# Seven block products where eight stood, in both squared-ReLU layers of a two-layer decoder trunk

## The chip, the cores and the metric

The kernel runs on one core of a Trainium2 chip. The metric is the device time of one execution in microseconds (us), as the median of several runs; 2941.45 us before the change (three runs, 2940.11 to 2944.54). Everything is float32. The matrix products run on TensorE (PE in the profile) in three passes: both operands are split into a high part (float32 rounded to the engine's float32r format) and a low part (the remainder), and high by high, high by low and low by high are added in the accumulator (PSUM).

## What is computed

Two layers over 1024 tokens of width 1024. Each has a token mixer (mLSTM with RG-LRU in layer 0, sliding-window attention in layer 1), a cross attention into 256 memory tokens, and the squared-ReLU layer that the change touches:

```python
D_MODEL = 1024; SEQ = 1024; D_FF = 4 * D_MODEL; DEPTH = 2

def squared_relu_mlp(u, w1, w2):
    return jnp.square(jax.nn.relu(u @ w1)) @ w2

for l in range(DEPTH):
    ...                                   # token mixer, then cross attention
    u = squared_relu_mlp(rms_norm(h, g_ff_pre[l]), w_ff1[l], w_ff2[l])
    h = h + rms_norm(u, g_ff_post[l])
```

## The kernel before

The whole trunk is one program. A tile has 128 partitions. The normalised input of a stage is kept transposed (channels on partitions) as u[half], one pair of tiles (`uh`, `ul`: high, low) for each half of 512 tokens, each of 8 blocks of 128 channels.

**Pools.** On-chip memory is cut into pools that live through the whole program: `xp` with 35 slots of 520 floats per partition for temporaries (`X`), `up` with four tiles of 8 by 512 (`U`), `hp` with four row tiles of 1024 (`H`), `wp` with three slots for raw weights (tag `wr`) and five for split weights (tag `w`), and eight accumulator banks in two pools, `pg` (three, `G`) and `pt` (five, `T`). A weight tile is loaded by `load_raw` (L354) and split by `split` (L210): ScalarE copies the high part (L211), VectorE subtracts it to get the low one (L212).

**Order.** Each engine runs its instructions in one order, which a list scheduler makes from the program's order and its own durations when the kernel is built: an instruction whose operands and slot are there goes ahead of an earlier one that has to wait. Two chains are fixed by hand with `ordered`: all TensorE instructions stand in program order (key "pe"), and so do the weight loads (key "w"). What has to come between matmuls is placed by a counter of estimated TensorE time, `clock`: `defer(d, fn)` puts a piece of work d us later, and `pe(us)` advances the counter and runs what is due. `ready(u)` runs all pieces that are left until u is complete.

**The squared-ReLU layer before** (`mlp`, L700 to L757). The hidden width is taken in eight chunks of 512 (`for c in range(8)`). In each, `proj_T` (L387) makes four hidden tiles for each token half, 24 matmuls of 128x128 by 128x512 each (8 channel blocks, three passes) into one G bank; then ScalarE takes the ReLU (L717), VectorE multiplies it with the accumulator to square it (L718), and `split` makes `hh` and `hl`, which stay on the chip in X slots. Then `tile_out` adds the chunk's share of the output for 8 token tiles by 2 column halves, 12 matmuls each, with `hh`/`hl` as the stationary operand; VectorE adds the bank to the running sum `acc` (L738; a ScalarE copy, L736, in the first chunk). The last chunk's products are mixed with the output's normalisation: after each tile `post_half` (L333: ScalarE sums squares, GpSimd multiplies by the gain, L337) and, after the second half of a token tile, `post_norm` (L339: `rsqrt` on VectorE, L253 to L265, two residual updates, L345, and the store). In layer 0, `after` starts the next layer's `pre_norm` (L305) for the first four token tiles.

In both layers that makes 8 x 4 x 2 x 24 = 1536 matmuls in the first product and 8 x 16 x 12 = 1536 in the second.

`pre_norm` sums squares, scales, and after a planned delay transposes a token tile on TensorE (`transposed`, L287, L86 in the trace), multiplies by the gain (L296, `ut`), and splits into `uh` (ScalarE, L299) and `ul` (GpSimd, L300). The layer's second half of tokens is normalised this way while the first chunk's products of the first half run.

Of the kernel before, what the change touches and what calls it, by code (L numbers as in the profile page):

```python
# [10 lines left out]
F32 = mybir.dt.float32  # L11
# [17 lines left out]
NX = 35  # L29
NH = 4  # L30
XW = 520
# [28 lines left out]
def trunk(ctx: ExitStack, tc, a, out, stop=99):  # L60
# [32 lines left out]
    up = ctx.enter_context(tc.tile_pool(name="up", bufs=NU))  # L93
    hp_ = ctx.enter_context(tc.tile_pool(name="hp", bufs=NH))
    xp = ctx.enter_context(tc.tile_pool(name="xp", bufs=NX))
# [3 lines left out]

    ctr = [0]  # L100
# [87 lines left out]
    def X(shape=(P, HALF), dt=F32, n="x"):  # L188
        assert int(np.prod(shape[1:])) <= XW
        return xp.tile(list(shape), dt, tag="x", name=nm(n))  # L190
# [4 lines left out]
    def U(shape=(P, 8, HALF), n="u"):  # L195
        return up.tile(list(shape), F32R, tag="u", name=nm(n))
# [29 lines left out]

    cst = cp.tile([P, 288], F32, name="cst")
# [74 lines left out]

    left = {}

    def pre_norm(h, g, u, t, delay, where=None):  # L305
# [10 lines left out]
        def rest(un):  # L316
            transposed(un, [(g, u[0][:, :, c], u[1][:, :, c])])
            left[id(u)] -= 1
# [63 lines left out]
    def mm3(ps, lh, ll, rh, rl, start, stop):  # L382
        mm(ps, lhsT=lh, rhs=rh, start=start, stop=False)
        mm(ps, lhsT=lh, rhs=rl, start=False, stop=False)
        mm(ps, lhsT=ll, rhs=rh, start=False, stop=stop)
# [313 lines left out]

    def mlp(l, u, hsrc, hdst, after):  # L700

        W1, W2 = a["w_ff1"][l], a["w_ff2"][l]
        acc = [[None, None] for _ in range(8)]
        wpool[0] = 0
        g = None
        for c in range(8):
            hid = [[None, None] for _ in range(4)]
            ng = 4 if c == 0 else 2
            for n0 in range(0, 4, ng):
                ws = [load_w(w_cols(W1, (4 * c + n0 + j) * P), (8, P)) for j in range(ng)]  # L710
                for half in range(2):
                    if c == 0:
                        ready(u[half])
                    for j in range(ng):
                        ps = proj_T(ws[j], u[half])
                        r = H(n="rl")[:, 0:HALF]
                        act(out=r, in_=ps, func=AF.Relu)  # L717
                        vec.tensor_tensor(out=r, in0=ps, in1=r, op=ALU.mult)  # L718
                        hh, hl = X(dt=F32R, n="hh"), X(dt=F32R, n="hl")
                        split(hh, hl, r)  # L720
                        hid[n0 + j][half] = (hh, hl)
                        pe(0)

            def w2(n):
                return [load_w(w_rows(W2, 4 * c + 2 * q, 2, n * HALF, HALF), (2, HALF)) for q in range(2)]

            def tile_out(t, n, ws):
                lhs = []
                for k in range(4):
                    hh, hl = hid[k][t // 4]  # L730
                    s = slice((t % 4) * P, (t % 4 + 1) * P)
                    lhs.append((hh[:, s], hl[:, s]))
                ps = proj_lhs(ws, lhs)
                if c == 0:
                    acc[t][n] = X(n="acc")
                    act(out=acc[t][n], in_=ps, func=AF.Copy)  # L736
                else:
                    vec.tensor_tensor(out=acc[t][n], in0=ps, in1=acc[t][n], op=ALU.add)  # L738
                pe(0)

            if c < 7:
                for n in range(2):
                    ws = w2(n)
                    for t in range(8):
                        tile_out(t, n, ws)
            else:
# [7 lines left out]
                for t, n in order:  # L754
# [3 lines left out]
                    if n == 1:  # L758
                        h = post_norm(acc[t], ss, hsrc, hdst, t)
                        if after is not None:  # L760
                            after(t, h)
# [761 lines left out]
```

## Time and profile before

| | |
|---|---|
| median of three runs | 2941.45 us (2940.11 to 2944.54) |
| the profiled execution's own time | 2938.32 us |
| its span, first to last instruction | 2936.5 us |
| mean granted TensorE clock | 0.982 of full speed |
| TensorE matmuls busy | 2816.4 us (96%), 13518 instructions |
| VectorE busy | 1617.2 us (55%) |
| ScalarE busy | 1139.1 us (39%) |
| GpSimd busy | 548.8 us (19%) |
| moved | 274.29 MB, mean 93 GB/s |

Views that are quoted below. The page's part 5 and the lists of groups give line, engine, operation, output<-inputs (for a matmul the moving operand first, then the stationary one), the count, then the busy time in us, the mean ns of one, the engine's idle time before them and what ended it. The timeline gives start and duration in us, and in brackets the idle time of the engine before the instruction and what ended it. Windows give the stretch, its length, the busy us of PE, PEld (weight loads), DVE (VectorE), ACT (ScalarE) and POOL (GpSimd) with their instruction counts, the granted clock, the DMA share and GB/s.

The busy time of matmuls overlaps between neighbours: one is shown as 0.39 us long, and the next starts before it ends. The pace is read from start to start. The squared-ReLU layer of layer 0 runs from 831.82 us to about 1553 us, that of layer 1 ends the program.

### The profile page before, as it was taken

What the parts mean: (1) busy time and instruction counts of PE and PEld (TensorE: products, weight loads), DVE (VectorE), ACT (ScalarE), POOL (GpSimd) and SP (SyncE); (2) the same over time, 40 slices, a digit from 0 to 9 for tenths busy, and PEclk for the clock granted to TensorE, in tenths of its full rate; (3) what the DMA queues carried; (4) which work ended last, traced back from release to release, by engine and by line L of the source; (5) the groups of instructions that cost most, each with busy time, mean ns of one, the idle gap of its engine ahead of it and who ended that gap; (6) DMA issues with size and microseconds to landing.
All of it is one profiled execution on the core that took longest, in us unless ns stands there. A gap on an engine that the chain in (4) does not pass through costs nothing. (4 is left out here: it accounts for less than half of the span.)

```text
span 2936.5 us, 35526 instructions
## 1 busy us (share of the span) xinstructions
PE 2816.4 (96%) x13518; PEld 2340.3 (80%) x13518; DVE 1617.2 (55%) x3168; ACT 1139.1 (39%) x2271; POOL 548.8 (19%) x442
## 2 busy tenths in 40 slices
PE   8999999999999999999998889879999999999998
PEld 8988778878788888888877668668888888888886
DVE  7776586656662333333367966986655233333336
ACT  5455454445443112221134764754544311122212
POOL 1351243522110000000024451641211000000003
PEclk9999999899999999999999899989999999999999
DMA  8633542234331111111124154034432111111113
GB/s 255 192 90 105 176 129 79 87 132 166 97 110 56 44 43 58 44 44 57 44 92 153 50 158 154 26 94 163 146 101 94 44 52 49 43 53 48 44 50 115
DMA packets 265754, 274.29 MB, mean 93 GB/s; under 512 B 11784, under 2 KB 200688, under 8 KB 265584
## 3 DMA queue, kind: packets, MB, share of 16 engines
q1 hardware_dynamic: 265584, 272.03, 29.2%
q8 instruction: 106, 1.74, 0.2%
q14 instruction: 64, 0.52, 0.1%
HBM read 234.24 MB, written 37.75 MB: 93 GB/s over the span
## 5 line engine op out<-in xcount | busy, mean ns | idle before, releaser
L82 PE MATMUL g<-uh,w 128*128 128x512 f32 x3200 | 1009.6, 392 | 1.6 <-ACT uh L299 1.6
L82 PEld LDWEIGHTS g<-uh,w 128*128 128x128 f32 x3200 | 602.3, 188 | 126.2 <-ACT uh L299 2.5
L82 PE MATMUL g<-w,hh 128*128 128x512 f32 x2048 | 642.5, 395 | 1.4 <-DVE acc L738 1.4
L212 DVE TENSOR_TENSOR w<-wr,w 128x1024 fp32r<-128x1024 f32 x344 | 439.8, 1280 | 350.7 <-ACT w L211 349.6
L82 PE MATMUL g<-ul,w 128*128 128x512 f32 x1600 | 624.7, 390 | 1.7 <-POOL ul L300 1.7
L211 ACT ACTIVATE w<-wr 128x1024 fp32r<-128x1024 f32 x344 | 362.7, 1056 | 583.0 <-PE g L82 512.2
L82 PEld LDWEIGHTS g<-w,hh 128*128 128x128 f32 x2048 | 384.5, 188 | 92.0 <-DVE acc L738 1.8
L82 PE MATMUL g<-w,hl 128*128 128x512 f32 x1024 | 404.0, 395 | 0.0
L82 PEld LDWEIGHTS g<-ul,w 128*128 128x128 f32 x1600 | 301.2, 188 | 62.5 <-POOL ul L300 2.3
L738 DVE TENSOR_TENSOR acc<-g,acc 128x512 f32<-128x512 f32 x224 | 154.4, 689 | 299.7 <-PE g L82 298.3
L718 DVE TENSOR_TENSOR rl<-g,rl 128x512 f32<-128x512 f32 x128 | 88.5, 692 | 379.1 <-ACT rl L717 379.1
L337 POOL TENSOR_TENSOR acc<-acc,gain 128x512 f32<-128x512 f32 x32 | 44.5, 1396 | 1335.6 <-ACT junk L274 1335.6
L717 ACT ACTIVATE rl<-g 128x512 f32<-128x512 f32 x128 | 76.4, 597 | 427.9 <-PE g L82 425.2
L82 PEld LDWEIGHTS g<-w,hl 128*128 128x128 f32 x1024 | 192.4, 188 | 45.7
L300 POOL TENSOR_TENSOR ul<-ut,uh 128x512 fp32r<-128x512 f32 x96 | 136.3, 1440 | 403.0 <-ACT uh L299 401.9
L82 PE MATMUL g<-w,uh 128*128 128x512 f32 (+1 forms) x640 | 173.6, 361 | 10.7 <-DVE w L212 4.8
L82 PE MATMUL g<-w,pTh 128*128 128x512 f32 x512 | 161.1, 396 | 0.5 <-ACT pTh L211 0.5
L82 PEld LDWEIGHTS g<-w,uh 128*128 128x128 f32 x640 | 111.9, 194 | 25.7 <-DVE w L212 5.1
L82 PE MATMUL g<-w,ul 128*128 128x512 f32 (+1 forms) x320 | 114.0, 356 | 0.0
L212 DVE TENSOR_TENSOR hl<-rl,hh 128x512 fp32r<-128x512 f32 x128 | 89.3, 698 | 44.2 <-ACT hh L211 44.2
L82 PEld LDWEIGHTS g<-w,pTh 128*128 128x128 f32 x512 | 95.0, 188 | 21.7 <-ACT pTh L211 1.0
L82 PE MATMUL g<-w,pTl 128*128 128x512 f32 x256 | 101.2, 395 | 0.0
(326 smaller groups left out, 3820.7 us busy)
## 6 DMA issues: line engine op xcount, KB each, us to landing
wr<-in_w_ff SPq DMA_DIRECT2D x128, 512.0 KB, 3.9
h<-h SPq DMA_DIRECT2D x100, 512.0 KB, 3.7
wr<-in_ev_w_in SPq DMA_DIRECT2D x48, 512.0 KB, 3.6
wr<-in_w_xkv SPq DMA_DIRECT2D x32, 512.0 KB, 4.7
wr<-in_w_xq SPq DMA_DIRECT2D x32, 512.0 KB, 3.9
wr<-memv SPq DMA_DIRECT2D x32, 512.0 KB, 3.8
wr<-in_od_w_qkv SPq DMA_DIRECT2D x24, 512.0 KB, 4.3
h<-in_x SPq DMA_DIRECT2D x16, 512.0 KB, 4.4
```

The source lines that it names most:

```text
L82: ins = nc.tensor.matmul(*ar, **kw)
L211: act(out=h, in_=src, func=AF.Copy)
L212: (eng or vec).tensor_tensor(out=l, in0=src, in1=f(h), op=ALU.subtract)
L300: pool.tensor_tensor(out=ul[:, q], in0=t, in1=f(uh[:, q]), op=ALU.subtract)
L337: eng.tensor_tensor(out=dst, in0=y, in1=g[:, c], op=ALU.mult)
L717: act(out=r, in_=ps, func=AF.Relu)
L718: vec.tensor_tensor(out=r, in0=ps, in1=r, op=ALU.mult)
L738: vec.tensor_tensor(out=acc[t][n], in0=ps, in1=acc[t][n], op=ALU.add)
```

## The change

Both products of `mlp` become a 2x2 block scheme with seven block products and shared sums (Winograd's form of Strassen's scheme). The two blocks of the token dimension are the halves u[0] and u[1]; channels and hidden columns are cut in two as well.

- **First product.** 16 steps of two hidden tiles. A step loads two raw tiles (one into `wr`, the other into an H slot), splits two weight blocks as they are (`direct`), makes four sums of weight blocks on VectorE and splits five blocks (`sums`), and runs seven products of 12 matmuls (`product`). The four results are put together in the accumulator where two products share a bank (`more=True`: the second product adds to a bank that was read in between) and on VectorE. ReLU and square are two ScalarE instructions in place.
- **Sums of the input.** `transposed_sum` makes the first four blocks of u[1] hold a sum of three blocks from the start; `t_sum` makes the three other sums of the input, on VectorE and ScalarE, once per layer at step 0.
- **The hidden layer goes through memory.** The four blocks of the hidden layer and their sums (four more VectorE instructions) make seven left operands, which are stored to a DRAM tile `hid` (seven stores of 256 KB a step) and loaded back in the second product (`lefts`: two loads of 512 KB and a split for each block product).
- **Second product.** Four steps of seven products of 48 matmuls (4 token tiles by 4 blocks by three passes). Four blocks of W2 of 1 MB each are loaded a step; the right operands are three of them and four sums, split by `right`. `gather` adds banks to 20 running sums.
- **The output's normalisation** stands behind the last product, in a loop over eight token tiles, where it was mixed with the last chunk's products before; tiles 4 to 7 take two more VectorE additions each, tiles 0 to 3 one.
- **Pools.** `x` and `u` are opened and closed by phase: in the first product `t` (six tiles) and ten X slots take the old X pool's place, in the second `hl` (four tiles) and `b` (six) take the place of `u`, with 22 X slots. X slots are 520 floats wide up to layer 0's squared-ReLU layer and 512 from there on.

The diff, cut to its core ("..." marks what is left out):

```diff
-NX = 35
...
+NX = 34
...
-XW = 520
+XW = (520, 512)
+NX1, NX2 = 10, 22
...
+    def open_pool(key, n, side):
+        ctr[0] += 1
+        stage_pools[key] = tc.alloc_tile_pool(name=f"{key}{ctr[0]}", bufs=n, side=side, reuse_waits="tile")
+    def close_pool(*keys):
+        for key in keys:
+            stage_pools.pop(key).release()
...
+    def transposed_sum(un, g, u, first, c):
...
+        act(out=u[0][:, 4:8, c], in_=ts[1], func=AF.Copy)
+        pool.tensor_tensor(out=u[1][:, 4:8, c], in0=ts[1], in1=f(u[0][:, 4:8, c]), op=ALU.subtract)
+        s = ts[0]
+        vec.tensor_tensor(out=s, in0=ts[1], in1=s, op=ALU.subtract)
+        for b in first:
+            vec.tensor_tensor(out=s, in0=s, in1=f(b[:, 0:4, c]), op=ALU.add)
+        act(out=u[0][:, 0:4, c], in_=s, func=AF.Copy)
+        vec.tensor_tensor(out=u[1][:, 0:4, c], in0=s, in1=f(u[0][:, 0:4, c]), op=ALU.subtract)
...
+    def mm3(ps, lh, ll, rh, rl, start, stop, more=False):
...
+    hid = dp.tile([7, 16 * P, HALF], F32, name="hid")
...
+        def pair_raw(i):
...
+                ordered("w", nc.sync.dma_start(out=r, in_=w_rows(W1, 4 * j, 4, 2 * i * P, 2 * P)))
...
+        def direct(raws):
...
+            for j in range(2):
+                split(w[:, 0, j], w[:, 1, j], raws[j][:, :, 0:P])
...
+        def sums(raws):
...
+            s1 = X((P, 4, P), F32, "s1")
+            tt(s1, a21, a22, add)
+            tt(a21, a11, a21, sub)
+            tt(a11, s1, a11, sub)
+            tt(a12, a12, a11, sub)
...
+        def product(ps, w, j, b, k0, more=False):
...
+        def squared_relu(x, src):
+            act(out=x, in_=src, func=AF.Relu)
+            act(out=x, in_=x, func=AF.Square)
...
+        ready(u[0])
+        first = 2
...
+        ready(u[1])
+        close_pool("x")
+        xw[0] = HALF
+        open_pool("t", 6, "left")
+        open_pool("x", NX1, "left")
...
+        def t_sum(x, kx, y, ky):
...
+            h, lo = (stage_pools["t"].tile([P, 4, HALF], F32R, tag="t", name=nm("t")) for _ in range(2))
+            for k in range(4):
+                d, e = X(n="d"), X(n="e")
+                tt(d, f(x[0][:, kx + k]), f(y[0][:, ky + k]), sub)
+                tt(e, f(x[1][:, kx + k]), f(y[1][:, ky + k]), sub)
+                tt(d, d, e, add)
+                split(h[:, k], lo[:, k], d)
+            return h, lo
...
+        for i in range(16):
...
+            w23, w4a, w1 = sums(raws)
+            if i >= first:
+                b1 = G("b1")
+                product(b1, wa, 0, u[0], 0)
+                p1 = X(n="p1")
+                act(out=p1, in_=b1, func=AF.Copy)
+            b2 = G("b2")
+            product(b2, w23, 0, u[1], 0)
+            u2 = X(n="u2")
+            tt(u2, b2, p1, add)
+            pe(0)
+            if i >= first:
+                product(b1, wa, 1, u[0], 4, True)
+                c11 = X(n="c11")
+                squared_relu(c11, b1)
                 pe(0)
-            if c < 7:
+            if i == 0:
+                ts.append(t_sum(u[1], 0, u[0], 0))
+                ts.append(t_sum(u[1], 4, u[1], 0))
+                ts.append(t_sum(u[0], 4, u[1], 0))
+            t3, t1, t4 = ts
+            b3, b4 = T("b3"), T("b4")
+            product(b3, w23, 1, t3, 0)
+            c22 = X(n="c22")
+            tt(c22, b3, u2, add)
+            pe(0)
+            product(b4, w1, 0, t1, 0)
+            c21 = X(n="c21")
+            tt(c22, b4, c22, add)
+            squared_relu(c22, c22)
+            pe(0)
+            product(b3, w4a, 1, t4, 0, True)
+            tt(c21, b3, u2, add)
+            squared_relu(c21, c21)
+            pe(0)
+            product(b4, w4a, 0, u[1], 4, True)
+            c12 = u2
+            tt(c12, b4, u2, add)
+            squared_relu(c12, c12)
+            pe(0)
+            s = [H("s")[:, 0:D] for _ in range(2)]
+            s1, s2, s3, s4 = (s[j // 2][:, (j % 2) * HALF : (j % 2 + 1) * HALF] for j in range(4))
+            tt(s1, c12, c22, add)
+            tt(s2, s1, c11, sub)
+            tt(s3, c11, c12, sub)
+            tt(s4, c21, s2, sub)
+            for x, src in enumerate((c11, c21, s4, c22, s1, s2, s3)):
+                store(x, i, src)
+        close_pool("x", "t", "u")
+        open_pool("x", NX2, "left")
+        open_pool("hl", 4, "right")
+        open_pool("b", 6, "right")
+        def big(key, n, dt=F32):
...
+        def gather(key, t, ps):
...
+                acc[key, t] = X(n="acc")
+                act(out=acc[key, t], in_=ps, func=AF.Copy)
+            else:
+                tt(acc[key, t], ps, acc[key, t], add)
...
+        W2v = W2.rearrange("(i e q) n -> e q i n", e=2, q=P)
+        for c in range(4):
...
+                    b = big("b", "braw")
+                    ordered("w", nc.sync.dma_start(out=b, in_=W2v[e, :, 4 * c : 4 * c + 4, n * HALF : (n + 1) * HALF]))
+                    blocks.append(b)
+            b11, b12, b21, b22 = blocks
...
+            def right(src):
+                h, lo = big("hl", "th", F32R), big("hl", "tl", F32R)
+                split(h, lo, src)
+                return h, lo
...
+            def lefts(x):
+                h, lo = (wp.tile([P, 4, HALF], F32R, tag="w", name=nm("sh"), bufs=NW) for _ in range(2))
...
+                    nc.sync.dma_start(out=r, in_=hid[x, r0 : r0 + 2 * P, :].rearrange("(i q) t -> q i t", q=P))
+                    split(h[:, 2 * j : 2 * j + 2], lo[:, 2 * j : 2 * j + 2], r)
+                return h, lo
...
+            pa = banks("pa")
+            for t in products(0, right(b11), pa):
+                gather("u", t, pa[t])
+                pe(0)
+            t1, t2 = big("b", "t1"), big("b", "t2")
+            tt(t1, b12, b11, sub)
+            tt(t2, b22, t1, sub)
+            pb = banks("pb")
+            for t in products(5, right(t2), pb):
+                gather("u", t, pb[t])
+                pe(0)
+            r21 = right(b21)
+            tt(b21, b21, t2, sub)
+            tt(b12, b22, b12, sub)
+            for t in products(1, r21, pa, True):
+                gather("11", t, pa[t])
+                pe(0)
+            pb = banks("pb")
+            for t in products(4, right(t1), pb):
+                gather("22", t, pb[t])
+                pe(0)
+            pa = banks("pa")
+            for t in products(6, right(b12), pa):
+                gather("22", t, pa[t])
+                pe(0)
+            for t in products(2, right(b22), pb, True):
+                gather("12", t, pb[t])
+                pe(0)
+            for t in products(3, right(b21), pa, True):
+                gather("21", t, pa[t])
+                pe(0)
+        close_pool("b", "hl")
+        if after is not None:
+            open_pool("u", NU, "right")
+        g = gain(a["g_ff_post"][l], True)
+        sy = small(16, "sy", 1)
+        for t in range(8):
+            ss = sy[:, 2 * t : 2 * t + 2]
+            keys = ("11", "12") if t < 4 else ("21", "22")
+            y = [acc[key, t % 4] for key in keys]
+            for n in range(2):
+                if keys[n] != "11":
+                    tt(y[n], y[n], acc["u", t % 4], add)
+                post_half(y[n], y[n], g, ss, n, pool)
+            h = post_norm(y, ss, hsrc, hdst, t)
+            if after is not None:
+                after(t, h)
+            pe(N1)
+        if after is None:
+            drain()
+            close_pool("x")
+        else:
+            close_pool("x")
+            xw[0] = XW[1]
+            open_pool("x", NX, "left")
```

## Rows read from the trace of the kernel before

**Rows 1.** The page, part 1: busy us, share of the span, instructions.

```profile
PE 2816.4 (96%) x13518; PEld 2340.3 (80%) x13518; DVE 1617.2 (55%) x3168; ACT 1139.1 (39%) x2271; POOL 548.8 (19%) x442
```

**Rows 2.** Windows: busy us per engine (instructions), granted clock, DMA share, GB/s.

```profile
50.00:100.00 50.00, 50.00 (x422) 50.00 (x421) 37.65 (x68) 26.50 (x39) 9.27 (x6) 1.00 0.94 285
900.00:950.00 50.00, 50.00 (x220) 40.83 (x219) 11.33 (x13) 16.54 (x24) 0.00 (x0) 1.00 0.17 53
1565.00:1600.00 35.00, 34.77 (x157) 28.85 (x158) 26.55 (x72) 12.79 (x33) 10.64 (x14) 0.91 0.54 184
1650.00:1700.00 50.00, 37.40 (x177) 30.43 (x176) 45.72 (x113) 37.35 (x107) 19.04 (x17) 0.84 0.28 96
```

**Rows 3.** The page, part 5: groups: busy us, mean ns, idle before.

```profile
L82 PE MATMUL g<-uh,w 128*128 128x512 f32 x3200 | 1009.6, 392 | 1.6 <-ACT uh L299 1.6
...
L212 DVE TENSOR_TENSOR w<-wr,w 128x1024 fp32r<-128x1024 f32 x344 | 439.8, 1280 | 350.7 <-ACT w L211 349.6
...
L738 DVE TENSOR_TENSOR acc<-g,acc 128x512 f32<-128x512 f32 x224 | 154.4, 689 | 299.7 <-PE g L82 298.3
...
L337 POOL TENSOR_TENSOR acc<-acc,gain 128x512 f32<-128x512 f32 x32 | 44.5, 1396 | 1335.6 <-ACT junk L274 1335.6
```

**Rows 4.** Timeline, PE, first product, layer 0: start us, us, instruction.

```profile
1103.31 0.39 PE L82 MATMUL g<-ul,w 128*128 128x512 f32 x1
...
1122.35 0.39 PE L82 MATMUL g<-ul,w 128*128 128x512 f32 x1
```

**Rows 5.** Timeline, PE, second product (layer 1).

```profile
2895.60 0.40 PE L82 MATMUL g<-w,hl 128*128 128x512 f32 x1
...
2916.55 0.40 PE L82 MATMUL g<-w,hl 128*128 128x512 f32 x1
```

**Rows 6.** Timeline, PE, output projection of the mixer, U tiles stationary.

```profile
622.04 0.39 PE L82 MATMUL g<-w,yl 128*128 128x512 f32 x1
...
636.32 0.39 PE L82 MATMUL g<-w,yl 128*128 128x512 f32 x1
```

**Rows 7.** Timeline, ACT, POOL, DVE: last tiles of the second half, layer 0.

```profile
834.63 0.58 ACT L274 ACTIVATE junk<-g 128x512 f32<-128x512 f32 x1
...
858.20 2.52 POOL L300 TENSOR_TENSOR ul<-ut,uh 128x512 fp32r<-128x512 f32 x2 [1.91 <-ACT uh L299]
...
847.87 1.28 DVE L296 TENSOR_TENSOR ut<-tr,col 128x512 f32<-128x512 f32 x2
```

**Rows 8.** Timeline, PE, start of the layer, layer 0.

```profile
831.82 0.39 PE L82 MATMUL g<-uh,w 128*128 128x512 f32 x1
...
858.17 0.50 PE L82 MATMUL g<-uh,w 128*128 128x512 f32 x1 [0.81 <-ACT uh L299]
```

**Rows 9.** Timeline, PE, the last matmul of the program.

```profile
2924.23 0.40 PE L82 MATMUL g<-w,hl 128*128 128x512 f32 x1
```

**Rows 10.** Timeline, DVE, one output normalisation of the cross attention.

```profile
816.67 0.20 DVE L257 TENSOR_SCALAR rs<-sy 128x1 f32<-128x1 f32 x1
...
818.57 1.42 DVE L345 SCALAR_TENSOR_TENSOR h<-y,rs,h 128x512 f32<-128x512 f32 x2
```

**Rows 11.** Timeline, DVE, two like instructions of one rsqrt.

```profile
1549.11 1.20 DVE L264 SCALAR_TENSOR_TENSOR rs<-rs 128x1 f32<-128x1 f32 x1
...
1553.10 0.16 DVE L264 SCALAR_TENSOR_TENSOR rs<-rs 128x1 f32<-128x1 f32 x1
```

**Rows 12.** Timeline, PE, end of the layer in layer 0.

```profile
1526.83 1.27 PE L86 MATMUL tr<-cst,un 128*128 128x128 f32 x8 [1.79 <-ACT junk L274]
...
1555.41 0.73 PE L82 MATMUL g<-w,uh 128*128 128x512 f32 x2 [2.26 <-DVE acc L738]
...
1565.23 0.79 PE L82 MATMUL g<-w,uh 128*128 128x512 f32 x1 [4.75 <-DVE w L212]
```

**Rows 13.** The page, part 6: DMA issues, KB each, median us to landing.

```profile
wr<-in_w_ff SPq DMA_DIRECT2D x128, 512.0 KB, 3.9
```

**Rows 14.** Waits of the DMA queue: waiter, releaser, us in total, times, longest.

```profile
SPq L359 <- DVE w L212: 1907.5, 272, 50.1
```

More of the change, by code (lines that the diff above doesn't have):

```diff
@@ new lines, in wtile @@
+        def wtile(n):
+            return wp.tile([P, 2, 2, 4, P], F32R, tag="w", name=nm(n), bufs=NW)
+        def direct(raws):
+            w = wtile("w")
+            for j in range(2):
+                split(w[:, 0, j], w[:, 1, j], raws[j][:, :, 0:P])
+            return w
+        def sums(raws):
+            (a11, a21), (a12, a22) = [(r[:, :, 0:P], r[:, :, P : 2 * P]) for r in raws]
+            s1 = X((P, 4, P), F32, "s1")
[3 more added lines that the diff above has]
+            tt(a12, a12, a11, sub)
+            out = []
+            for r in raws:
+                w = wtile("w")
+                split(w[:, 0], w[:, 1], r.rearrange("p k (b n) -> p b k n", b=2))
+                out.append(w)
+            w = wtile("w1")
+            split(w[:, 0, 0], w[:, 1, 0], s1)
+            return out + [w]
@@ new lines, in product, with store @@
+        def product(ps, w, j, b, k0, more=False):
+            for k in range(4):
+                mm3(
+                    ps, w[:, 0, j, k], w[:, 1, j, k], b[0][:, k0 + k], b[1][:, k0 + k], k == 0 and not more, k == 3, more
+                )
+                if k < 3:
+                    pe(0.68)
+                else:
+                    clock[0] += 0.68
+        def squared_relu(x, src):
+            act(out=x, in_=src, func=AF.Relu)
+            act(out=x, in_=x, func=AF.Square)
+        def store(x, i, src):
+            nc.sync.dma_start(out=hid[x, i * P : (i + 1) * P, :], in_=src)
@@ new lines, in mlp @@
+        ready(u[0])
+        first = 2
+        pre = []
+        for i in range(first):
+            raws = pair_raw(i)
+            pre.append([raws, direct(raws), G("b1")])
+        p1s, c11s = H("p1"), H("c11")
+        for i in range(first):
+            product(pre[i][2], pre[i][1], 0, u[0], 0)
+            pre[i].append(p1s[:, i * HALF : (i + 1) * HALF])
+            act(out=pre[i][3], in_=pre[i][2], func=AF.Copy)
+            pe(0)
+        for i in range(first):
+            product(pre[i][2], pre[i][1], 1, u[0], 4, True)
+            pre[i].append(c11s[:, i * HALF : (i + 1) * HALF])
+            squared_relu(pre[i][4], pre[i][2])
+            pe(0)
@@ new lines, in mlp @@
+        ts = []
+        for i in range(16):
+            if i < first:
+                raws, wa, b1, p1, c11 = pre[i]
+            else:
+                raws = pair_raw(i)
+                wa = direct(raws)
+            w23, w4a, w1 = sums(raws)
[13 more added lines that the diff above has]
+                squared_relu(c11, b1)
+                pe(0)
+            if i == 0:
[30 more added lines that the diff above has]
+                store(x, i, src)
@@ L764, in trunk @@
+        if after is None:
+            drain()
+            close_pool("x")
+        else:
+            close_pool("x")
+            xw[0] = XW[1]
+            open_pool("x", NX, "left")
     W_in = a["ev_w_in"][0]
@@ L1457, in trunk @@
                 in_steps(rope_tables(), 3, 3.5)
-            cross(l, half, ux[half], hm, hxr, lambda t, h, u=u: pre_norm(h, gf, u, t, UD, "x"), None if half else mid)
+            cross(l, half, ux[half], hm, hxr, lambda t, h, u=u, first=uf[0] if half else None: pre_norm(h, gf, u, t, UD, "x", first), None if half else mid)
         if stop == 2 + 3 * l:
```

121 lines of the change are left out of this document (59 added, 62 removed).

## The prediction, made before the changed kernel was run

> **What bounds the kernel now.** I read the shares first: TensorE is busy 96% of the span, the next engine 55% [rows 1]. Then the windows of 50 us: inside a squared-ReLU layer TensorE has 50.00 of 50 busy at clock 1.00, while VectorE has 11.3 and DMA a share of 0.17 [rows 2]. So the layer is bound by the number of matmuls times their pitch, and a matmul fewer gives its whole pitch back, as long as nothing else starves TensorE. The groups say the same: 3200 matmuls of one kind waited 1.6 us in all [rows 3]. Other stages look different: at 1650 to 1700 us VectorE is busy 45.7 of 50, TensorE 37.4, and the clock falls to 0.84 [rows 2]. The question is how much of the new layer looks like that.
>
> **Pitch.** First product: from 1103.31 to 1122.35 us stand 84 matmuls, 19.04 us, 0.2267 each [rows 4]. Second product: 2895.60 to 2916.55, 90 matmuls, 20.95 us, 0.2328 each [rows 5]. The longer pitch goes with a stationary operand in an X slot of 520 floats: with a U tile as the stationary one, 63 matmuls take 14.28 us, 0.2267 [rows 6]. The new second product takes its stationary operand from a `w` slot, as the first does, so I use 0.2267 there too; bounds 0.2267 and 0.2328.
>
> **What is removed.** Per layer 2 x 1536 matmuls: 1536 x 0.2267 + 1536 x 0.2328 = 705.8 us. After: 16 x 7 x 12 = 1344 and 4 x 7 x 48 = 1344, so 2688 x 0.2267 = 609.4. Gain 96.4 a layer, 193 in all (88 a layer from the missing products, 8 from the pitch, so 177 if that does not come).
>
> **Steady work of VectorE.** A 512-float VectorE instruction takes 0.69 us alone [rows 3], and 0.60 behind another one: two take 1.28 [rows 7]. A 1024-float subtraction takes 1.28 [rows 3]. A step of the first product has 16 of 512 floats (two of the direct split, four weight sums, the split of the third weight tile, five additions of banks, four sums of hidden blocks) and two of 1024: 16 x 0.67 + 2 x 1.28 = 13.3 us beside 84 x 0.2267 = 19.0 of TensorE. A step of the second product has 28 additions of banks (0.69), 14 splits of 1024 (1.28), and 7 splits and 4 sums of 2048 floats, which the trace does not have: 4 x 0.60 = 2.40 to 2 x 1.28 = 2.56; I take 2.45. Sum 19.3 + 17.9 + 27.0 = 64 us beside 76 of TensorE. Both fit, but at 70% and 84%, where it is 23% now. [...] DMA has 1 MB of weights and 1.8 MB of stores per 19 us, then 4 MB and 7 MB per 76 us: some 150 GB/s, where the core has moved 285 [rows 2]. I charge the steady part 4 us a layer for the first product (0 to 16) and 3 for the second (0 to 10).
>
> **The start of the layer, the largest cost.** Now the last block of u[1] is complete at 858.20 + 2.52 = 860.7 us, 29 us after the first matmul at 831.82, and TensorE hardly waits, since four 24-matmul groups of the first half cover it; two gaps of 0.8 us are left, one is shown [rows 7, 8]. After the change only four products (48 matmuls, 10.9 us) and the transposes (3 us) stand ahead of the wait, so TensorE is out of work at 846. The sums in `transposed_sum` add four VectorE instructions a tile, but the products' planned distance no longer delays the last tile, whose input came at 834.63 [rows 7]: I take 858 (852 to 862). From then on VectorE has the weight sums of step 0 (5.5 us), and the three `t_sum`: 48 instructions of 0.60 to 0.69, 31 us. TensorE's order is fixed, so it follows the blocks as they come: the sixth product of step 0 ends at about 898, the seventh at 901, and step 1 waits for its own weight sums until 903. By then 9 products (24.5 us) and 3 us of transposes are done in 71 us: 43 idle, less the old 1.7. Some of the 11 us of weight sums fits into VectorE's earlier gaps: **38 us a layer** (25 if all of it does and u[1] comes at 852, 48 if none and 862).
>
> **Between the products.** W2's blocks (1 MB, 3.7 us at 285 GB/s [rows 2]) go to places that `u` held, and must be split (a ScalarE copy, then 2.45 on VectorE, together about 4.4) before the first product. If the first block's place was u[0]'s, the load is hidden and 4 us stay; if u[1]'s, load and split stand bare and the second product waits for three more blocks: 17. I take **10 a layer**.
>
> **The output's normalisation.** Before, it lay under the last chunk's matmuls; the program ended 11.9 us after the last matmul's end at 2924.6 [rows 9]. A token tile costs VectorE 1.9 us of rsqrt and 1.42 of updates [rows 10] and one or two additions, about 4.3, and GpSimd two multiplications of 1.4 [rows 3], while which VectorE is held up: one instruction of an rsqrt took 1.20 us beside GpSimd's, 0.16 without [rows 11]. I take 5.6 a tile. Tiles 0 to 3 can start when the sixth product's banks are added, so about two of eight fit under the seventh; six remain: 33.6 and the store 3, 36.6. **Layer 1: +24** (13 to 31). In layer 0 four tiles must also pass `pre_norm` (rsqrt, scaling, two multiplications: 3.7 each on VectorE) before the next layer's first matmul, behind five or six output tiles: 38 us (27 to 48). Before, that place had idle gaps of 12.6 us in seven pieces, three are shown [rows 12], and 4 us of transposes now hide in the wait: **layer 0: +21** (10 to 31).
>
> **Clock.** After 4.75 idle us before 1565.23 [rows 12] the stretch 1565 to 1600 was granted 0.91, which is 35 x 0.09 = 3.2 us [rows 2]. Four or five new places: **12** (0 to 20).
>
> **Sum.** 2 x 38 + 2 x 10 + 2 x 7 + 24 + 21 + 12 = 167. Against the profiled execution's 2938.3: 2938.3 - 193 + 167 = 2912. That execution lies 3.1 below the median, so **2915 us**.
>
> **Rivals.**
> *VectorE starves the first product (slower).* Three times a step a product adds to a bank that VectorE or ScalarE has to read first, and only one other product, 2.7 us, lies between; before, banks rotated and the groups did not wait [rows 3]. If a split of 1.28 us stands ahead of the two VectorE readings and the weights come late, 3.7 us a step are lost: 32 x 3.7 = 118, less the 8 counted: 3025. It decides from (2941 - 2915 + 8)/32 = 1.1 us a step. For it: 70% busy, splits that wait for ScalarE. Against it: the scheduler's order lets the readings go first. Chance 0.2. [...]
> *The gaps are filled (faster).* The lower ends: 2 x 25 + 2 x 4 + 10 + 13 and 6 of clock are 87, which gives 2938.3 - 193 + 87 + 3 = 2835 with no steady charge; a quarter of the way back to the forecast 2855. For it: none of that work needs TensorE, and the scheduler may put it into gaps. Against it: `t_sum` alone keeps VectorE 31 us, with 11 us of products to fill them. Chance 0.22.
> *The round trip through memory is not hidden (slower).* Loads stand on the same queue as stores that wait for VectorE; if each step's load (3.9 us [rows 13]) and split (2.3) followed the step before, 28 x 6.2 = 174: 3090. Against it: now loads wait for a free slot 1907 us in all, so they run far ahead [rows 14]. Chance 0.08.
> *The gain is eaten up (no change).* If the costs come to 193, 26 us more than I sum, say 47 at each start and 14 before each second product, the result is 2941; this lies within the forecast's own spread.
>
> **How the numbers follow.** Forecast 0.5 (2885 to 2955), of which 0.36 is faster, 0.08 within and 0.06 slower by more than 0.2% (5.9 us, about what a measurement can tell from no change). The faster rival adds 0.22, the starving one 0.01 within and 0.19 slower, the memory one 0.08: faster 0.58, same 0.09, slower 0.33. The range leaves out the memory rival and the far half of the starving one: 2845 to 2990.
>
> **What would show it.** In each layer's start VectorE near full for some 40 us while TensorE idles until 858 and is then fed in pieces; after it 220 matmuls per 50 us at clock 1.00 in both products, the second product's pitch at 0.227; a gap of 4 to 17 us before the first matmul of the second product; some 36 us after the last matmul of the program. The forecast is wrong if windows inside the first product show fewer than 210 matmuls per 50 us, if the gap at the start is under 25 or over 50, or if the tail is below 25.

## The result and the profile after

The changed kernel takes 3188.05 us (median of 4 runs, 3184.13 to 3190.69) against 2940.78 before on the same chip (2938.90 to 2944.54): ratio 1.0838, 95% interval 1.0819 to 1.0857. It is slower by 247 us, where 2915 was forecast. The profiled execution took 3187.12 us, its span is 3185.3.

Part 1 of the page, shares, answering [rows 1]:

```profile
PE 2772.4 (87%) x12750; PEld 2238.4 (70%) x12750; DVE 2096.9 (66%) x3672; ACT 1389.1 (44%) x2535; POOL 536.3 (17%) x434
```

TensorE has 768 matmuls fewer, as the change says, but its busy time fell by 44 us only and its idle time grew by more than 290. Windows of 50 us (busy us per engine with instructions, granted clock, DMA share, GB/s), answering [rows 2]; the first is the start of layer 0's first product, the second its middle, the third the second product, the fourth the end of layer 0:

```profile
850.00:900.00 50.00, 25.03 (x58) 12.50 (x56) 45.67 (x73) 15.05 (x24) 4.44 (x3) 0.61 0.06 21
1000.00:1050.00 50.00, 38.75 (x150) 29.86 (x149) 24.90 (x35) 17.35 (x26) 0.00 (x0) 0.86 0.34 116
1350.00:1400.00 50.00, 50.00 (x216) 40.27 (x215) 32.18 (x25) 24.88 (x27) 0.00 (x0) 1.00 0.48 162
1650.00:1700.00 50.00, 22.73 (x92) 18.25 (x92) 43.52 (x110) 19.05 (x48) 25.46 (x20) 0.66 0.44 150
```

The second product is full. The middle of the first product is not: 150 matmuls in 50 us where the forecast wanted 220, and VectorE has 25 of 50. So it isn't a lack of VectorE time. Part 5 of the page (groups: busy us, mean ns, idle before and who ended it) names the releaser; before, the 3200 matmuls of this kind waited 1.6 us in all [rows 3]:

```profile
L83 PE MATMUL b<-uh,w 128*128 128x512 f32 x1024 | 379.6, 443 | 192.5 <-ACT w L222 189.4
```

The timeline of one step (start us, us, engine, line; in brackets the idle time before and its end), TensorE, VectorE and ScalarE around 1010 us:

```profile
1011.69 0.40 PE L83 MATMUL b<-uh,w 128*128 128x512 f32 x1
1017.67 0.79 PE L83 MATMUL b<-uh,w 128*128 128x512 f32 x1 [5.58 <-ACT w L222]
1018.26 0.63 PE L83 MATMUL b<-ul,w 128*128 128x512 f32 x1
...
1009.32 0.69 DVE L756 TENSOR_TENSOR u<-b,u 128x512 f32<-128x512 f32 x1 [2.11 <-PE b L83]
1011.37 0.69 DVE L756 TENSOR_TENSOR s<-u,c 128x512 f32<-128x512 f32 x1 [1.36 <-ACT u L809]
...
1013.31 0.69 DVE L756 TENSOR_TENSOR s<-c,s 128x512 f32<-128x512 f32 x1
1013.91 0.68 DVE L756 TENSOR_TENSOR s<-wr,wr 128x512 f32<-128x512 f32 x1
...
1015.84 0.69 DVE L756 TENSOR_TENSOR wr<-s,wr 128x512 f32<-128x512 f32 x1
...
1012.90 0.63 ACT L222 ACTIVATE w<-wr 128x512 fp32r<-128x512 f32 x1 [1.56 <-DMA wr<-in_w_ff]
1016.56 2.00 ACT L222 ACTIVATE w<-wr 128x1024 fp32r<-128x1024 f32 x2 [2.54 <-DVE wr L756]
```

Here is the loss. The step's last product ends; VectorE adds its bank (1009.32), ScalarE squares, VectorE makes the four sums of hidden blocks (1011.37 to 1014.00), and only then, back to back, the weight sums of the next step (from 1013.91), whose split on ScalarE ends at 1017.6. TensorE has meanwhile only the one product that needs no sum, 2.7 us, until 1011.9, and starts again at 1017.67. From one start to the next 5.98 us pass in place of 0.23, and the matmuls behind the wait come at 0.43 to 0.67 us for some 4 us more. In layer 0 such a wait comes in each of the last 14 steps of the first product, every 27.1 to 27.3 us (the last start before it is at 930.15, 957.24, 984.45, 1011.69 ...), where 84 matmuls are 19.4. TensorE's granted clock is 0.50 of full speed from 1017.70 to 1021.70, and 0.86 in the window of 1000 to 1050.

Two causes are possible: the place of the weight sums on VectorE's list, or the load that they read. SyncE's queue, same step:

```profile
1005.85 3.04 SPq L812 DMA_DIRECT2D hid<-c  x2
1008.99 0.38 SPq L765 DMA_DIRECT2D wr<-in_w_ff  x1
1012.10 3.22 SPq L812 DMA_DIRECT2D hid<-s  x4
```

The load issued at 1008.99 stands behind stores that wait for ScalarE, and lands just before 1012.90, where ScalarE picks it up; the weight sums that read it start at 1013.91. The two causes lie 1 us apart, and the profile alone can't say which one counts.

The other places where TensorE waits: the start of the layer (868.67 to 912.51, where step 1 begins), between the products, the end of layer 0; then the last matmul (answering [rows 8, 9, 12]).

```profile
868.67 0.80 PE L83 MATMUL b<-uh,w 128*128 128x512 f32 x1 [15.61 <-ACT w L222]
...
903.13 2.47 PE L83 MATMUL b<-t,w 128*128 128x512 f32 x5 [5.49 <-DVE c L756]
...
912.51 0.50 PE L83 MATMUL b<-uh,w 128*128 128x512 f32 x1 [0.84 <-ACT w L222]
...
1324.18 0.80 PE L83 MATMUL pa<-th,sh 128*128 128x512 f32 x1 [14.56 <-ACT th L222]
...
1642.57 0.40 PE L83 MATMUL pa<-th,sh 128*128 128x512 f32 x1
1661.56 1.97 PE L87 MATMUL tr<-cst,un 128*128 128x128 f32 x8 [18.59 <-ACT junk L287]
...
1681.79 1.20 PE L83 MATMUL g<-w,uh 128*128 128x512 f32 x2
...
3151.18 0.40 PE L83 MATMUL pa<-th,sh 128*128 128x512 f32 x1
```

### The profile page after: what moved, and what is told of

Read it like the earlier page. It is cut to its first block, busy times and chain, and to the rows that moved or that the text cites. A ratio compares the mean times of both kernels' runs of the same rounds, so it can differ in the third digit from the quotient of the medians.

```text
span 3185.3 us, 35443 instructions
## 1 busy us (share of the span) xinstructions
PE 2772.4 (87%) x12750; PEld 2238.4 (70%) x12750; DVE 2096.9 (66%) x3672; ACT 1389.1 (44%) x2535; POOL 536.3 (17%) x434
## 5 line engine op out<-in xcount | busy, mean ns | idle before, releaser
L223 DVE TENSOR_TENSOR w<-wr,w 128x1024 fp32r<-128x1024 f32 (+1 forms) x344 | 399.8, 1171 | 229.6 <-ACT w L222 227.1
L83 PE MATMUL b<-uh,w 128*128 128x512 f32 x1024 | 379.6, 443 | 192.5 <-ACT w L222 189.4
L222 ACT ACTIVATE w<-wr 128x1024 fp32r<-128x1024 f32 (+1 forms) x344 | 332.3, 976 | 243.6 <-DVE wr L756 78.5
L83 PE MATMUL g<-uh,w 128*128 128x512 f32 x1152 | 378.9, 399 | 0.0
L83 PE MATMUL pa<-th,sh 128*128 128x512 f32 x1024 | 330.6, 400 | 29.0 <-ACT th L222 29.0
L83 PE MATMUL b<-t,w 128*128 128x512 f32 x1152 | 293.2, 409 | 24.9 <-DVE c L756 11.0
L83 PEld LDWEIGHTS g<-uh,w 128*128 128x128 f32 x1152 | 217.3, 189 | 49.5
L83 PE MATMUL pb<-th,sh 128*128 128x512 f32 x768 | 245.4, 396 | 0.0
L83 PE MATMUL g<-ul,w 128*128 128x512 f32 x576 | 228.2, 396 | 0.0
L83 PE MATMUL b<-ul,w 128*128 128x512 f32 x512 | 223.5, 437 | 0.0
```

The lines of the kernel that those rows point to most:

```text
L83: ins = nc.tensor.matmul(*ar, **kw)
L222: act(out=h, in_=src, func=AF.Copy)
L223: (eng or vec).tensor_tensor(out=l, in0=src, in1=f(h), op=ALU.subtract)
```

## The experiments

**Theories.** (A) *Place*: the weight sums stand behind the hidden sums on VectorE's list, so they are last whatever has landed. (B) *Load*: the second raw tile is loaded late, because it stands behind stores on SyncE's queue. (C) *Amount*: 13.3 us of VectorE work a step don't fit. Three kernels tell them apart; a fourth is for the second product's pitch, which was not 0.227 either.

**e1, the weights of the next step asked for ahead of the last two products.**

```
+            if i < 15:
+                raws = pre[i + 1][0] if i + 1 < first else pair_raw(i + 1)
+                ahead = None if i + 1 < first else direct(raws)
+                ahead = (ahead, sums(raws))
             product(b3, w4a, 1, t4, 0, True)
```

> The weights of step i+1 of the first product (loads, splits and the four weight sums) are asked for ahead of the last two block products of step i, not after its stores; on VectorE's list the sums now stand ahead of the hidden sums, and the second raw tile is loaded one step further ahead. Theory 'the weights of the next step come last' (either because VectorE has them behind the hidden sums, or because their load stands on the queue behind the stores of the step): the wait of 5.98 us a step goes, and with it the stretch at half clock behind it; a step goes from 27.1 to 19 to 20 us, 28 steps x 7 to 8 = 196 to 226 us less, 2962 to 2992. Rival 'VectorE has too much to do': 13.3 us a step stay, whatever their order; the step stays above 25 us, 3130 or more.

Measured: 2961.48 us (2959.34 to 2963.58), ratio to before 1.0065 (1.0050 to 1.0080). A window of the same stage:

```profile
1000.00:1050.00 50.00, 50.00 (x218) 40.64 (x217) 30.89 (x45) 22.32 (x36) 0.00 (x0) 1.00 0.50 169
```

and VectorE's timeline in it:

```profile
1010.89 0.69 DVE L756 TENSOR_TENSOR c<-b,u 128x512 f32<-128x512 f32 x1 [4.19 <-PE b L83]
1011.50 0.68 DVE L756 TENSOR_TENSOR s<-wr,wr 128x512 f32<-128x512 f32 x1
...
1021.59 0.69 DVE L756 TENSOR_TENSOR s<-u,c 128x512 f32<-128x512 f32 x1 [1.01 <-ACT u L809]
```

The weight sums now lie 10 us ahead of the hidden sums, between bank additions for which VectorE used to wait, and TensorE is full at 218 matmuls. The first product (first start to last end) went from 471.4 to 357.9 us in layer 0 and from 471.4 to 358.6 in layer 1: 226 of the 227 us. VectorE does the same work in it (386 instructions in layer 0, 272 us busy, in both kernels), so (C) falls.

**e2, slots of its own for the second raw tile, the text's order kept.**

```
-                    r = hp_.tile([P, 4, 2 * P], F32, tag="h", name=nm("wr"))
+                    r = own[i % 2].rearrange("p (k n) -> p k n", k=4)
...
-            s = [H("s")[:, 0:D] for _ in range(2)]
+            s = own[2:4] if own else [H("s")[:, 0:D] for _ in range(2)]
```

> Only the memory of the first product's rows of weights and hidden sums changes: the second raw tile of a step alternates between two tiles of its own, the two tiles of hidden sums are two others, where all of them took turns in one pool of four before. The text's order of the work is as it was. Theory 'the load of the second raw tile waits for a slot that holds hidden sums not yet stored': the load comes a step earlier, the weight sums with it, the step falls to 19 to 20 us, 2962 to 2992. Theory 'the order of the text puts the weight sums last': the step stays at 27 us, 3188. Theory 'VectorE has too much to do': 3188 too.

Measured: 2999.31 us (2998.56 to 3001.04), ratio 1.0194 (1.0179 to 1.0209). Windows:

```profile
900.00:950.00 50.00, 42.58 (x156) 32.89 (x156) 26.73 (x39) 17.80 (x27) 0.00 (x0) 0.85 0.25 89
950.00:1000.00 50.00, 44.38 (x183) 35.25 (x182) 28.86 (x42) 20.19 (x32) 0.00 (x0) 0.93 0.50 164
1000.00:1050.00 50.00, 50.00 (x218) 40.65 (x217) 33.59 (x49) 23.99 (x38) 0.00 (x0) 1.00 0.50 157
```

After two waits as before (933.72 and 961.36), the step is 19.4 us here too, as in e1; the early steps keep the time above the 2962 to 2992 that I expected. Nothing was reordered in the text, but on VectorE's list, which is fixed when the program is built, the weight sums moved ahead of the hidden sums:

```profile
1017.06 0.68 DVE L756 TENSOR_TENSOR s<-wr,own 128x512 f32<-128x512 f32 x1
...
1022.94 0.69 DVE L756 TENSOR_TENSOR own<-u,c 128x512 f32<-128x512 f32 x1
```

So the place on the list was itself a result of the shared slots.

**e3, the stores on GpSimd's queue.**

```
-            nc.sync.dma_start(out=hid[x, i * P : (i + 1) * P, :], in_=src)
+            nc.gpsimd.dma_start(out=hid[x, i * P : (i + 1) * P, :], in_=src)
```

> Only the queue of the hidden blocks' stores changes (GpSimd's instead of SyncE's); the order on VectorE stays, the weight sums behind the hidden sums. The loads no longer stand behind stores that wait for ScalarE. Theory 'the load that stands behind the stores is what comes last': it lands some 10 us earlier, the step falls to 20 us or so, 2970 to 3000. Theory 'VectorE's place for the sums is what comes last': the sums start at most 1 us earlier a step, since in the trace of the changed kernel the load lands 1 us ahead of the end of the hidden sums; 3160 to 3190.

Measured: 3189.04 us (3187.78 to 3191.96), ratio 1.0841 (1.0823 to 1.0859): no change. SyncE's queue, VectorE, TensorE of one step:

```profile
987.87 0.92 SPq L765 DMA_DIRECT2D wr<-in_w_ff  x2
...
999.55 0.69 DVE L756 TENSOR_TENSOR c<-b,u 128x512 f32<-128x512 f32 x1 [4.83 <-PE b L83]
...
1011.78 0.69 DVE L756 TENSOR_TENSOR s<-c,s 128x512 f32<-128x512 f32 x1
1012.39 0.69 DVE L756 TENSOR_TENSOR s<-wr,wr 128x512 f32<-128x512 f32 x1
...
1010.16 0.40 PE L83 MATMUL b<-uh,w 128*128 128x512 f32 x1
1016.15 0.79 PE L83 MATMUL b<-uh,w 128*128 128x512 f32 x1 [5.59 <-ACT w L222]
```

Two loads are now issued at 988, some 24 us ahead of the sums that start at 1012.39, and the wait is the same to 0.01 us, because the list still has the weight sums behind the hidden sums. (B) falls as the direct cause, (A) stands: the lateness of the load matters only through the list it leads to. VectorE keeps to its list here: it idles 4.83 us ahead of the bank addition at 999.55, 6 to 11 us after the loads were issued (such a load takes 3.8 us in the median in the changed kernel), and the weight sums still come only behind the hidden sums.

**e4, the sides of the memory swapped, every list of instructions unchanged.**

```
-        open_pool("hl", 4, "right")
+        open_pool("hl", 4, "left")
```

and so for each of the nine places where a pool is opened. The lists of all engines, and of the DMA issues, are the same as in the changed kernel.

> Only the sides of the memory change on which the pools of a phase are laid: what was laid from the upper end is laid from the lower one and the other way round; every engine's list of instructions is the same. In both traces a 128x512 product takes 227 ns where both operands lie below about 150 KiB of the partition and 232 to 235 ns where one lies above 156 KiB. Theory 'the place sets the pitch': u, yh, oh and th now lie at 90 to 155 KiB and take 227 ns, what lies in x goes to 232 ns; some 7600 products x 6.2 ns less, some 1500 x 4 more: 41 us less, about 3147; two of the six tiles of the block sums t end above 156 KiB and take 232. Rival 'the pitch hangs on the tile's role (which pool, stationary or moving)': no product changes, 3188.

Measured: 3167.38 us (3164.55 to 3169.57), ratio 1.0764 (1.0748 to 1.0780), 20.7 us below the changed kernel. A window of 280 us of second product, the changed kernel:

```profile
1340.00:1620.00 280.00, 280.00 (x1201) 225.18 (x1200) 197.35 (x175) 104.44 (x92) 0.00 (x0) 1.00 0.39 132
```

and e4:

```profile
1340.00:1620.00 280.00, 280.00 (x1237) 231.93 (x1236) 204.84 (x186) 104.33 (x92) 0.00 (x0) 1.00 0.41 134
```

280 / 1201 is 0.2331 us a matmul, 280 / 1237 is 0.2264. The place alone does it. The second product fell from 318.8 to 310.4 us in layer 0 and from 318.9 to 310.1 in layer 1, and the first layer's products start 5.4 us earlier (838.2 to 832.8; 831.82 before the change [rows 8]; this start spreads over 3 to 4 us between kernels that are the same up to there: 835.3 to 838.5 with the changed kernel's sides, 830.5 to 834.1 with the sides swapped). I expected twice as much in all (41 us): while the first product waits for the chain on VectorE, a shorter pitch in it gives nothing back (474.2 us in layer 0, 471.4 in the changed kernel).

**e5, e1 and e4 together.**

> The weight sums asked for early (as in e1) and the sides of the memory swapped (as in e4), together. Where the first product no longer waits, its own pitch is on the path: 48 of the 84 products of a step go from 233 to 227 ns, 24 (those of the block sums that come to lie high) from 227 to 233, so 0.14 us a step less; the second product 8.4 us a layer less and the work ahead of the first layer's products 5.4 us less, both as e4 showed. 5 + 17 + 5 = 27 us less than e1: 2930 to 2940. If only the second product's pitch counted: 2944.

Measured: 2935.06 us (2931.74 to 2936.85), ratio 0.9968 (0.9956 to 0.9980): 0.3% below the kernel before, little, but the interval leaves out 1. TensorE's timeline in the first product, a run of products with u between products with the block sums t, in e1:

```profile
1007.95 8.35 PE L83 MATMUL b<-t,w 128*128 128x512 f32 x36
1016.13 0.40 PE L83 MATMUL b<-uh,w 128*128 128x512 f32 x1
...
1027.34 0.85 PE L83 MATMUL b<-t,w 128*128 128x512 f32 x3
```

and in e5:

```profile
1006.29 8.56 PE L83 MATMUL b<-t,w 128*128 128x512 f32 x36
1014.69 0.39 PE L83 MATMUL b<-uh,w 128*128 128x512 f32 x1
...
1025.60 0.63 PE L83 MATMUL b<-t,w 128*128 128x512 f32 x2
```

48 products with u take 11.21 us in e1 and 10.91 in e5, 0.2335 and 0.2273; the 36 with t go the other way, 8.18 (0.2272) to 8.40 (0.2333). u moved from the upper end (160 to 224 KiB of the partition) to 90 to 154 KiB, t to the upper end (176 to 224), by the allocation of each kernel's tiles. So it is neither role nor pool. All six t tiles came to lie high, not two as I wrote.

**e6, no block sums** (blocks of u[1] in their place).

```
-                ts.append(t_sum(u[1], 0, u[0], 0))
...
+                ts = [v[1], v[0], v[1]]
```

> e1 with the three sums of the activations' blocks left out (blocks of u[1] stand in their place, so what is computed is not the reference's). This prices the start of the layer: in e1's trace TensorE comes out of work at 850 us, waits 15.9 us for the first weight sums behind u[1], 4.3 us for the first block sum, then gets the blocks in pieces until 894 and waits 6.1 us more. Theory 'the chain of block sums on VectorE sets the second half of the start': 871 to 900 shrinks to the 8 us that the 36 products take, 21 us and the time at half clock behind them less a layer, 42 to 52 us in all, 2910 to 2920. Rival 'TensorE would wait for the weights anyway': 15 us or less in all, 2946 or more.

Measured: 2924.68 us (2922.46 to 2925.84), ratio 0.9934 (0.9919 to 0.9949), 36.8 us below e1, where 42 to 52 were expected. The first product fell from 357.9 to 335.5 us, so the block sums cost 22 us a layer, as worked out (21); but the second grew from 318.7 to 328.0: it now starts before the rows of `hid` are back, and waits 6.8 and 2.8 us for its left tiles (ended by ScalarE's and VectorE's split of them). So it gives 9 us back, less the 5 by which the wait ahead of it shrank (14.4 to 9.4).

**e7, rows 0 to 3 beside the last two products.** In the last round the products run 0, 5, 1, 4, 2, 6, 3, and

```
+                for t in products(6, right(b12), pa):
...
+                    if ROWS[l]:
+                        row_out(t)
```

> e1, and in the last of the four rounds of the second product the seven products are taken in another order (those that close the upper rows first), so that rows 0 to 3 are normalised, added and stored while the last two products run; in the first layer the next layer's norm reads these rows back. Theory 'the ends are the row work alone, and it can lie beside products': 4 of 8 rows leave the last stretch (34.1 us in e1), 14 to 17 us less in the second layer, and 6 to 10 us of the 18.6 before the first transposes in the first layer: 2934 to 2942. Rival 'VectorE has no room beside the products': the splits of the last product come late by what the rows take, at most 5 us gained, 2956 or more.

Measured: 2964.26 us (2961.73 to 2965.88), ratio 1.0068 (1.0053 to 1.0083): nothing gained on e1. The tail, from the last matmul to the end, fell from 34.1 to 29.3 us, where 14 to 17 less were expected. In layer 0 the last matmul of the second product was followed by 43.6 us (1527.93 to 1571.57) up to the next layer's projection, where e1 had 39, with the rows read back. The rival's number came, but not its way: the second product took no longer (318.1 and 318.6 us; 318.7 and 318.6 in e1). GpSimd and VectorE in the stretch beside the last two products show one cost of the rows there:

```profile
2910.64 11.11 POOL L378 TENSOR_TENSOR acc<-acc,gain 128x512 f32<-128x512 f32 x7 [646.36 <-ACT junk L288]
...
2915.84 0.93 DVE L277 SCALAR_TENSOR_TENSOR rs<-rs 128x1 f32<-128x1 f32 x1
2916.69 0.14 DVE L272 TENSOR_SCALAR rs<-rs 128x1 int32<-128x1 int32 x1
...
2918.07 2.45 DVE L277 SCALAR_TENSOR_TENSOR rs<-rs 128x1 f32<-128x1 f32 x2
...
2921.95 0.14 DVE L278 SCALAR_TENSOR_TENSOR rs<-rs 128x1 f32<-128x1 f32 x1
```

Instructions of one element a partition that read two tensors (SCALAR_TENSOR_TENSOR) mostly take 0.93 to 1.20 us, or 2.45 for two, while GpSimd multiplies rows by the gain (until 2921.75), and 0.14 to 0.21 once it is done, as [rows 11] showed in another place. Those with one tensor and numbers (TENSOR_SCALAR) take 0.14 to 0.20 beside it. That this alone keeps the gain so small isn't shown.

**e8, e5 and e7 together.**

> e5 and e7 together: sums asked for early, sides swapped, rows 0 to 3 beside the last two products. If the parts add up, 2961 - 27 - 23 = 2911 (2900 to 2920), below the kernel before. If the rows beside the products cost as much as they gain, 2934.

Measured: 2935.67 us (2933.88 to 2936.89), ratio 0.9974 (0.9963 to 0.9985): as e5, and as the second number that I gave (2934).

**e9, e5 with the 12 additions of the shared sum made ahead of the last products.**

```
+                if c == 3:
+                    for t in range(4):
+                        tt(acc[key, t], acc[key, t], acc["u", t], add)
```

(`key` is "22", "12" and "21" in turn, behind products 1, 4 and 6 of the last round's 0, 5, 1, 4, 6, 2, 3.)

> e5, and the 12 additions of the shared partial sum to the output's tiles, which e5 makes after the last product of each layer, are made in the last round ahead of the last products (4 each behind the products with which the shared sum, the upper right and the lower left corner no longer wait for it). Theory 'the ends are VectorE's row work': 12 x 0.69 = 8.3 us leave VectorE's list behind the last product; the tail of the second layer falls from 34.4 to 26 to 28 us, the wait behind the first layer's last product (39 us in all) by 2 to 4, since only the upper four rows' four additions lie ahead of it: 2922 to 2928. Rival 'VectorE's small instructions beside GpSimd set the row's time, whatever is added': tail 33 us or more, 2932 or more.

Measured: 2933.53 us (2927.98 to 2934.56), ratio 0.9966 (0.9953 to 0.9979). The tail went from 34.4 to 32.3 us, not to 27. Neither of my two theories gives this. Taking 8.3 us off VectorE's list left what was there in e5 too: two updates of h that take 3.29 us in place of 1.42 (3.50 and 3.37 in e5), and then a wait at the end. In the changed kernel two such updates at 3165.61 take 3.50 us and two at 3172.99 take 3.37, beside GpSimd's multiplications (3163.16 to 3168.56 and 3172.89 to 3175.82), and two at 3169.71, between these, 1.41. The updates in e9:

```profile
2910.86 3.29 DVE L385 SCALAR_TENSOR_TENSOR h<-acc,rs,h 128x512 f32<-128x512 f32 x2
...
2921.11 1.42 DVE L385 SCALAR_TENSOR_TENSOR h<-acc,rs,h 128x512 f32<-128x512 f32 x2 [0.77 <-DMA h<-h]
2924.11 1.42 DVE L385 SCALAR_TENSOR_TENSOR h<-acc,rs,h 128x512 f32<-128x512 f32 x2 [1.59 <-DMA h<-h]
```

The last rows wait for their own h, whose load lands late (0.77 and 1.59 us; 1.46 in e5). That GpSimd alone sets the row's time isn't shown.

**e10, e9 with e7's order, rows 0 to 3 early in the second layer alone.**

> e9, and in the second layer alone the upper four rows are normalised and stored beside the last two products, as e7 did in both. e7's trace gave 4.6 us of the tail for it there and lost as much and more in the first layer, where the rows were read back. If that adds up: tail 22 to 25 us, 2917 to 2925. If the additions had been the only thing that could lie beside products: same as e9.

Measured: 2918.03 us (2915.50 to 2920.46), ratio 0.9920 (0.9903 to 0.9936). Tail 24.1 us, as expected, and from layer 0's last product to layer 1's first it takes 699.4 us (704.7 in e9). The new order with the rows early in both layers (e8 against e5) and the additions by themselves (e9 against e5) gave 2 us or less; the new order, the additions and the rows early in one layer only give 17 together. What each of the three gives within them no run separates. This is the fastest version: 0.8% below the kernel before, 8.5% below the changed one.

## Why the prediction was wrong

**The step that failed is the steady work of VectorE in the first product**, charged 4 us a layer with an upper bound of 16. It cost 113, in waits (471.4 us for the first product against e1's 357.9). I compared amounts, 13.3 us of VectorE against 19.0 of TensorE, and they do fit. I didn't follow the one chain that runs from a step's last product to the next step's second one: bank addition 0.69, relu and square 1.3, four hidden sums 2.6, three of the weight sums and a split among them 2.6, ScalarE's split 1.06: 8.3, and 8.4 from 1009.32 to 1017.67 with the gaps, against 2.7 us of TensorE's work. 8.4 less 2.7 is the 5.7 us that are seen. VectorE's prices in it stood in the working, ScalarE's on the page of before (597 ns for a ReLU of 512, 1056 ns for a split of 1024), and the diff has the sums at the head of a step, behind the stores.

**The rivals.** "VectorE starves the first product" named the engine and a loss of 3.7 us a step, but for the banks, on which the product waits only once in each layer, at its start (5.49 us at 903.13); I held against it that the order would let the readings go first. From step 1 on the order did, and put the weight sums last. "The round trip through memory" named the load behind the stores, 6.2 us a step and 3090, and comes nearest to the result; e3 shows that its queue is not what delays the step. What delays it is the place of the sums on the list, and that place changed when the load no longer shared slots with the hidden sums (e2). Against it I held the long waits for slots before [rows 14]; they told of the slots of before, not of slots that loads and results share.

**Pitch.** Wrong, with the wrong reason. 0.2331 in the second product, not 0.2267; it isn't the X slot but the place in the partition (e4, e5). Before, `w` lay at 32 to 72 KiB, u at 72 to 136 and X from 152 KiB up, and [rows 4 to 6] go with that: 0.2267 with both operands in `w` and u, 0.2328 with `hl` in X; the change moved u to 160 to 224 KiB, and th and tl to 192 to 224. Per layer 1344 x 0.2331 + 16 x (48 x 0.2335 + 36 x 0.2272) = 623.5 where 609.4 was summed: 28 us for both layers, and some 6 ahead of the first.

**Start of the layer.** The mechanism held: u[1] and the first weight sums (a wait of 15.6 us), then the block sums in pieces. Step 1 starts at 912.51, 74 us after the first product (838.21), where 71 were worked out (903 from 831.82). The working lacks one wait, the 5.49 us at 903.13 for a bank that VectorE reads behind the block sums on its list. In e1, where no later step waits, the first product takes 358 us for 310 of matmuls: 48, against 43 (the 38, and 5 of transposes and old gaps that were there before). The granted clock from 850 to 900 is 0.61 in the changed kernel, 0.50 from 868.70 to 874.00 and from 878.40 to 897.00.

**Between the products**: 14.6 us, and 5.5 more in the second product (318.8 for 1344 x 0.2331 = 313.3), 20, against 10 + 3. The gap is near the upper end of its range (17): the loads of W2's blocks follow the last stores on SyncE's queue.

```profile
1312.64 3.22 SPq L812 DMA_DIRECT2D hid<-s  x4
1315.97 2.50 SPq L929 DMA_DIRECT2D braw<-in_w_ff  x4
```

I had asked only for the place that the blocks go to, not for their place in the queue; which of the two holds the loads back isn't shown.

**Second product's steady work**: right, 216 matmuls per 50 us beside a VectorE that is 58 to 80% busy. **Ends**: right; the tail is 33.7 us (36.6), the wait in layer 0 39.2 (38).

So of the 275 us between the sum (2912) and the profiled execution (3187), 218 are the waits of the first product (226 less the 8 charged), 34 the pitch, 24 the starts of both products (10 and 14), less 12 of clock that these contain and 2 at the ends; some 13 are not assigned. Some 7 of them may lie in layer 1 ahead of its first product (665.1 us from its first projection, 658.2 before); no run looked there. Without the failed step's waits and with most of the pitch back, e5 lands at 2935.

## What to carry to other kernels

Two engines whose work fits side by side in amount can still wait for each other in every step (here 13.3 us of VectorE beside 19.0 of TensorE, which idles 5.58 us before 1017.67): follow the chain from a step's last result to the next step's first need, in the order in which the engine's list has it, and hold it against what the waiting engine has left to do. In this kernel it paid to ask for the next step's work ahead of the current step's finishing work (e1), and to give its loads slots that they don't share with that step's results (e2). When pools are moved, look at the pitch of the operations that read them (0.2331 and 0.2264 us here, by the place alone).

## What the runs showed of the hardware

With the same list of instructions, a 128x512 matmul takes 0.2264 to 0.2273 us with both operands in the lower part of the partition (up to 154 KiB; th and tl in e4, u in e5) and 0.2331 to 0.2335 with the moving one in the upper part (from 160 KiB; th and tl in the changed kernel, u in e1, t in e5). Before, the stationary operand made the same difference: 0.2328 [rows 5] in X slots, from 152 KiB up, against 0.2267 [rows 4]. Why the place counts is open: no run looked for the cause or for the exact border.
